# The first branch's half of the output mix in seven block products for eight, with block sums of y made by GpSimd

## The chip, the cores and the metric

The kernel runs on one core of a Trainium2 chip. The metric is the device time of one execution in microseconds (us). A core has five engines that each work through a list of instructions in order and wait for each other by semaphores: TensorE (PE, matrix products; its weight loads are shown as PEld), VectorE (DVE), ScalarE (ACT), GpSimd (POOL) and SyncE (SP, which starts most of the DMA transfers). SBUF is the memory that all of them work on, PSUM the one into which TensorE writes its products.

## The reference

One block of a network on x of 1024 rows by 1024 columns, batch 1. Two attention branches of 512 columns each are projected to 1024 columns, multiplied by gates and added:

```python
h = rms_norm(x, g_pre_mix[l])
proj = h @ w_in[l]
...
gates = jax.nn.sigmoid(proj[..., c1:].astype(jnp.float32)).astype(x.dtype)
gate_sb, gate_diff = jnp.split(gates, N_BRANCHES, axis=-1)
y_sb = stick_breaking_attention(sb_q.reshape(sb_shape), sb_k.reshape(sb_shape), sb_v.reshape(sb_shape))
...
y_diff = (rms_norm(y_diff, w_subln[l]) * (1.0 - lam_init)).reshape(b, s, DIFF_WIDTH)
merged = gate_sb * (y_sb @ w_sb_out[l]) + gate_diff * (y_diff @ w_diff_out[l])
x = x + rms_norm(merged @ w_o[l], g_post_mix[l])
h = rms_norm(x, g_pre_mlp[l])
u = jnp.square(jax.nn.relu(h @ w_up[l]))
x = x + rms_norm(u @ w_down[l], g_post_mlp[l])
```

## The kernel before

**Arithmetic.** All is float32. A product of two float32 matrices is made of three TensorE products of halves: each operand is split into a part `hi`, rounded by ScalarE to the format that TensorE takes (a cast, shown as CAST or COPY), and `lo`, the rest (a subtraction, shown as TENSOR_TENSOR of VectorE); hi·hi, hi·lo and lo·hi are added in PSUM. So every new operand costs one ACT and one DVE instruction before TensorE can use it.

**Stages.** x is normalised and transposed; then come eight attention units, u = 0 to 3 stick-breaking (each two heads) and u = 4 to 7 differential. While a unit's attention runs, a generator (`fill`) hands out other work for TensorE between its blocks: the projections of the next unit and the products of the gates. In the last unit (h = 3, u = 7) this filler is `last_products`: four pairs of gate blocks, each pair as seven block products for eight. A pair needs sums of its weights (`pair_sums`, four GpSimd instructions of 128x512 on the pages `fw`, L593 to L596), their splits (`split_pair`, L603 and L604), and block sums T1 to T4 of the transposed h, which were made in earlier units, stored to DRAM, and are loaded and split here (`split_sum`, L577 and L580). Its products go to the PSUM tiles `g_b`, `g_d`, `g_c` (L547), and VectorE adds them (L631, L641, L645, L649, L653).

In the attention itself, for a block of rows, `z` is the tile of scores (L273, L274); VectorE adds the bias and finds the minimum (`low`, L414), ScalarE takes exponentials, VectorE combines the two maps (`s`, L432), TensorE transposes the result into `tr_df` (L292), ScalarE and VectorE split it into `wth` and `wtl` (L298, L299), and TensorE multiplies by v into `av_d`. At the end of a group of blocks `finish_diff` normalises (`sq`, L387 to L389) and stores y to `y_dram`.

**The mix.** The results y of the units are loaded from `y_dram` as hi and lo. For each of eight blocks b of 128 output columns, `half_mix(b, i, tag)` loads half of the weights (i = 0 for the stick-breaking branch, y 0 to 3; i = 1 for the differential one, y 4 to 7), splits them (`wmix`, L752 and L753), loads the gate, applies its sigmoid (L728), and makes 4 × 3 × 2 = 24 matmuls of 128x512 (L762). 16 halves are 384 matmuls. `merge` multiplies the two by their gates (L773), adds them (L775) and splits the sum for the next stage (L776, L777), the product with w_o (L872).

**The order** on each engine isn't the order of the code: a scheduler that plans with a model of the times sorts the whole program's instructions before it runs. On the chip each engine then keeps to that order. Where a tile goes is set by pools: a tile waits until an older one of its tag and place is done with. The weights of `last_products` and of the mix share the tag `w` with four places, their raw rows the tag `raw` with two.

## Time and profile before

| | |
|---|---|
| three runs | 1453.62, 1453.90 and 1456.99 us, median 1453.9 |
| profiled execution | 1453.24 us, of which the span of the trace is 1451.5 us |
| granted TensorE clock | 0.999 of full speed |
| last attention unit, its second half | 560 to 647 us from the start of the span |
| mix | 647 to 736 us |

A row of the groups on the page reads: line of the kernel, engine, operation, the tile written `<-` the tiles read, shape, count, then busy time, mean length in ns of one, and the engine's idle time just before them with what ended most of it. A row of the timeline has the start in us from the span's start, the length, engine, line, operation, tiles, shape and count, and in brackets the idle time of the engine before it and what released it. A row of the waits has who waited `<-` for what, us in total, number, longest.

### The profile page before, as it was taken

How to read it: one execution, taken by the hardware profiler on the slowest of the kernel's cores; microseconds unless marked ns; L12 is line 12 of the kernel's file. 1: busy time of each engine (PE TensorE's matmuls, PEld its weight loads, DVE VectorE, ACT ScalarE, POOL GpSimd, SP SyncE). 2: the span in 40 equal slices, each digit the busy share in tenths (PEclk: the TensorE clock that was granted, in tenths of full speed). 3: DMA queues.
4: the chain of work that ended last, by engine and by line, in shares of the span. 5: the costliest groups of instructions: out<-in, count | busy, mean ns of one | idle time of the engine just before them, and what ended most of it. 6: DMA issues, size and time to landing. Idle time of an engine off the chain costs nothing. (4 is left out here: it accounts for less than half of the span.)

```text
span 1451.5 us, 19994 instructions
## 1 busy us (share of the span) xinstructions
PE 1425.8 (98%) x7238; PEld 1209.1 (83%) x7238; DVE 1017.3 (70%) x1352; ACT 751.4 (52%) x1325; POOL 388.4 (27%) x377
## 2 busy tenths in 40 slices
PE   7999999999999999999999999999999999999997
PEld 6888998899889888788888878888888888888886
DVE  5477998788657777854755489766664669764783
ACT  6465665666656776444534465444444443534350
POOL 2012322234125002210002334333330357232611
PEclk9999999999999999999999999999999999999999
DMA  5432312222323247475657736544446785678681
GB/s 207 111 94 66 77 48 81 66 73 70 110 94 109 82 153 240 153 277 179 190 167 234 238 129 208 177 159 145 139 159 200 263 276 180 211 236 285 191 288 58
DMA packets 100283, 233.09 MB, mean 161 GB/s; under 512 B 9964, under 2 KB 25560, under 8 KB 100184
## 3 DMA queue, kind: packets, MB, share of 16 engines
q1 hardware_dynamic: 85784, 211.89, 46.2%
q10 hardware_dynamic: 14400, 19.93, 3.8%
q8 instruction: 57, 0.93, 0.3%
q14 instruction: 42, 0.34, 0.1%
HBM read 160.45 MB, written 65.29 MB: 156 GB/s over the span
## 5 line engine op out<-in xcount | busy, mean ns | idle before, releaser
L356 DVE TENSOR_TENSOR_SCAN rest<-rest 128x896 f32<-128x896 f32 (+3 forms) x64 | 88.1, 1385 | 16.4 <-POOL rest L351 15.6
L351 POOL TENSOR_SCALAR_AFFINE_SELECT rest<-rest 128x128 f32<-128x128 f32 x64 | 26.5, 414 | 242.4 <-ACT rest L347 242.4
L762 PE MATMUL mix<-y,wmix 128*128 128x512 f32 x384 | 88.2, 390 | 0.2 <-DMA y<-y_dram 0.2
L762 PEld LDWEIGHTS mix<-y,wmix 128*128 128x128 f32 x384 | 71.9, 188 | 15.4 <-DMA y<-y_dram 0.6
L824 DVE TENSOR_TENSOR lS_lo<-raw_S,lS_hi 128x1024 fp32r<-128x1024 f32 x32 | 53.9, 1683 | 40.1 <-ACT lS_hi L817 40.1
L1170 PE MATMUL dS<-rT_hi,lS_hi 128*128 128x512 f32 x192 | 74.7, 389 | 0.0
L1170 PE MATMUL dS<-rT_lo,lS_hi 128*128 128x512 f32 x192 | 74.7, 389 | 0.0
L1170 PE MATMUL dS<-rT_hi,lS_lo 128*128 128x512 f32 x192 | 74.7, 389 | 0.0
L817 ACT CAST lS_hi<-raw_S 128x1024 fp32r<-128x1024 f32 x32 | 33.6, 1051 | 74.5 <-DMA raw_S<-s_dramS 40.7
L419 ACT ACTIVATE s<-s,low 128x896 f32<-128x896 f32 (+7 forms) x64 | 49.7, 777 | 40.4 <-DVE low L414 40.0
L347 ACT ACTIVATE rest<-z 128x512 f32<-128x512 f32 (+2 forms) x96 | 48.1, 501 | 27.7 <-PE z L274 19.8
L299 DVE TENSOR_TENSOR wtl_sb<-tr_sb,wth_sb 128x512 fp32r<-128x512 f32 (+1 forms) x80 | 48.0, 628 | 8.5 <-ACT wth_sb L298 8.1
L298 ACT CAST wth_sb<-tr_sb 128x512 fp32r<-128x512 f32 (+1 forms) x80 | 41.2, 555 | 24.5 <-PE tr_sb L292 24.1
L351 POOL TENSOR_SCALAR_AFFINE_SELECT beta<-beta 128x128 f32<-128x128 f32 x64 | 52.2, 816 | 2.7 <-ACT beta L348 1.9
L414 DVE CUSTOM_DVE_ANT_0 s<-z,bias 128x512 f32<-128x512 f32 (+3 forms) x64 | 37.3, 586 | 21.1 <-PE z L274 14.9
L207 PE MATMUL acc_gate<-h,hi_gate 128*128 128x512 f32 x128 | 50.6, 396 | 0.0
L208 PE MATMUL acc_gate<-h,lo_gate 128*128 128x512 f32 x128 | 50.5, 394 | 0.0
L206 PE MATMUL acc_gate<-h,hi_gate 128*128 128x512 f32 x128 | 50.4, 394 | 0.0
L994 PE MATMUL c<-hB_lo,wa_hi 128*128 128x512 f32 x128 | 49.9, 390 | 0.0
L994 PE MATMUL c<-hB_hi,wa_hi 128*128 128x512 f32 x128 | 49.9, 390 | 0.0
L1170 PE MATMUL dA<-rB_hi,lA_hi 128*128 128x512 f32 x128 | 49.8, 389 | 0.0
L1170 PE MATMUL dA<-rB_lo,lA_hi 128*128 128x512 f32 x128 | 49.8, 389 | 0.0
(397 smaller groups left out, 4814.1 us busy)
## 6 DMA issues: line engine op xcount, KB each, us to landing
s_dramS<-us SPq DMA_DIRECT2D x64, 256.0 KB, 4.1
raw_S<-s_dramS SPq DMA_DIRECT2D x32, 512.0 KB, 4.1
s_dramA<-u ACTq DMA_DIRECT2D x48, 256.0 KB, 2.3
raw_A<-s_dramA SPq DMA_DIRECT2D x24, 512.0 KB, 4.3
y<-y_dram SPq DMA_DIRECT2D x16, 512.0 KB, 5.2
g<-gate_dram SPq DMA_DIRECT2D x16, 512.0 KB, 4.5
raw_up<-in_w_up_dram SPq DMA_DIRECT2D x16, 512.0 KB, 4.0
up<-in_w_up_dram SPq DMA_DIRECT2D x16, 512.0 KB, 4.0
```

What stands on the lines that cost most here:

```text
L206: nc.tensor.matmul(acc, w_hi[:, ks], b_hi, start=(k == 0), stop=False)
L207: nc.tensor.matmul(acc, w_hi[:, ks], b_lo, start=False, stop=False)
L208: nc.tensor.matmul(acc, w_lo[:, ks], b_hi, start=False, stop=(k == NK - 1))
L299: nc.vector.tensor_tensor(lo[:, :n], tr[:, :n], f32(hi[:, :n]), op=ALU.subtract)
L347: nc.scalar.activation(rest[:, c0:c1], z, AF.Sigmoid, scale=-1.0)
L351: nc.gpsimd.affine_select(tl[:, dg], tl[:, dg], pattern=[[-1, P]], compare_op=ALU.is_gt, fill=fill, base=0, channel_multiplier=1,)
L356: nc.vector.tensor_tensor_scan(back, back, back, 1.0, op0=ALU.mult, op1=ALU.bypass)
L419: e = nc.scalar.activation(s[:, :nk], s[:, :nk], AF.Exp, bias=low, scale=-1.0, accum_out=sums[:, m:m + 1],)
L762: nc.tensor.matmul(accs[c], st, mv[:, cs], start=(first and k == 0), stop=(last and k == 3))
L824: nc.vector.tensor_tensor(lo, raw, f32(hi), op=ALU.subtract)
L994: nc.tensor.matmul(acc, st[:, ks], mv, start=(first and k == 0 and i == 0), stop=(k == 3 and i == 2), skip_group_check=True,)
L1170: nc.tensor.matmul(acc, st[:, e, ts], mv[:, e, :], start=(first and e == 0 and i == 0), stop=(last and e == 1 and i == 2))
```

## The change

Of the first branch's half of the mix, blocks 2 to 7 are made in three pairs, (2, 3), (4, 5) and (6, 7). A pair of blocks is a product of a 2x2 by a 2x2 matrix of blocks (two blocks of output columns, two halves of the 512 inner columns; two halves of the rows), made with seven products of sums in place of eight products. Each of the seven has 2 × 3 = 6 matmuls of 128x512, so a pair has 42 in place of 48. Blocks 0 and 1 and the whole second half stay as they are.

For this, four things are added.

- Each stick-breaking unit also stores its y before the split (`y_raw_dram`, 16 stores of 128 KB).
- `form_y_sums`, called twice in `last_products`, loads these (4 loads of 512 KB), makes four sums each time with GpSimd (8 instructions of 128x512), and stores them to `ty_dram` (8 stores of 256 KB).
- In the mix, `split_ty` loads the sums (8 loads of 256 KB) and splits them; `pair_weights` makes sums of the weights (4 GpSimd instructions of 128x256 a pair) and splits those.
- `pair_products` adds products in PSUM and SBUF with VectorE, and `gated` multiplies by the gates, one product by VectorE and three by GpSimd.

The loads of y 4 to 7, and of all gates but the first two, are put behind the loads of the first pair's weights, and the weights of the first pair and of two second halves are made ahead.

```diff
+            nc.sync.dma_start(out=raw_rows[:, :, j % 2, :], in_=part)
...
+        def form_y_sums(k):
+            if k == 0:
+                page_in["ys"] = pa.tile([P, 4, HALF], F32, tag="v", name="y_sums", bufs=3)
+            ys = page_in["ys"]
+            for j in range(2):
+                nc.sync.dma_start(
+                    out=ys[:, 2 * j:2 * j + 2, :], in_=y_raw_dram[2 * j + k].rearrange("p (c n) -> p c n", c=2)
+                )
+            b11, b12, b21, b22 = (ys[:, i, :] for i in range(4))
+            for name, dst, x0, x1 in (
+                ("T1", b11, b12, b11), ("T3", b12, b22, b12), ("T2", b22, b22, b11), ("T4", b21, b21, b22)
+            ):
+                nc.gpsimd.tensor_tensor(dst, x0, x1, op=ALU.subtract)
+                nc.sync.dma_start(out=ty_dram[name][:, k, :], in_=dst)
...
                 if n < 2:
                     nc.sync.dma_start(out=v, in_=p1_dram[n + 2])
+                    form_y_sums(n)
...
+        def split_ty(name, hi, lo):
+            for k in range(2):
+                nc.sync.dma_start(out=f32(lo[k]), in_=ty_dram[name][:, k, :])
+            for k in range(2):
+                nc.scalar.copy(hi[k], f32(lo[k]))
+                nc.vector.tensor_tensor(lo[k], f32(lo[k]), f32(hi[k]), op=ALU.subtract)
+            ty[name] = hi, lo
...
+        def pair_weights(b):
+            raw = stream.tile([P, 2, HALF], F32, tag="raw", name=f"raw_pair{b}")
+            for e in range(2):
+                last_pair[0] = nc.sync.dma_start(out=raw[:, e, :], in_=w_mix[b + e][:, 0:HALF])
+            wa = wide_tile(f"wa_mix{b}")
+            nc.scalar.copy(wa[:, 0, :], raw[:, 0, :])
+            nc.vector.tensor_tensor(wa[:, 1, :], raw[:, 0, :], f32(wa[:, 0, :]), op=ALU.subtract)
...
+            nc.gpsimd.tensor_tensor(s1, a21, a22, op=ALU.add)
+            nc.gpsimd.tensor_tensor(a21, a11, a21, op=ALU.subtract)
+            nc.gpsimd.tensor_tensor(a11, s1, a11, op=ALU.subtract)
+            nc.gpsimd.tensor_tensor(a12, a12, a11, op=ALU.subtract)
+            hi, lo = (wide_tile(f"w_{n}_mix{b}") for n in ("hi", "lo"))
+            nc.scalar.copy(hi, raw)
+            nc.vector.tensor_tensor(lo, raw, f32(hi), op=ALU.subtract)
+            nc.scalar.copy(w1[:, 0, :], s1)
+            nc.vector.tensor_tensor(w1[:, 1, :], s1, f32(w1[:, 0, :]), op=ALU.subtract)
...
+            product_y(a, first(0), "B11")
+            nc.scalar.copy(v, a)
+            product_y(acc_b, quarter(0, 0), "T2")
+            nc.vector.tensor_tensor(v, acc_b, v, op=ALU.add)
+            product_y(d, quarter(1, 0), "T3")
+            nc.vector.tensor_tensor(q, d, v, op=ALU.add)
+            product_y(a, first(1), "B21", first=False)
+            product_y(c, (w1[:, 0, :], w1[:, 1, :]), "T1")
+            nc.vector.tensor_tensor(q, c, q, op=ALU.add)
+            product_y(d, quarter(1, 1), "T4", first=False)
+            nc.vector.tensor_tensor(r, d, v, op=ALU.add)
+            product_y(c, quarter(0, 1), "B22", first=False)
+            nc.vector.tensor_tensor(v, c, v, op=ALU.add)
+            def gated():
+                g0, g1 = load_gate(b, 0), load_gate(b + 1, 0)
+                left, right = slice(0, HALF), slice(HALF, S)
+                nc.vector.tensor_mul(g0[:, left], a, g0[:, left])
+                nc.gpsimd.tensor_mul(g0[:, right], v, g0[:, right])
+                nc.gpsimd.tensor_mul(g1[:, left], r, g1[:, left])
+                nc.gpsimd.tensor_mul(g1[:, right], q, g1[:, right])
+                return [g0, g1]
...
+        gated = pair_products(2)
         for b in range(NK):
+            if b in (4, 6):
+                gated = pair_products(b)
+            if b > 1 and b % 2 == 0:
+                sbs += gated()
+            df = half_mix(b, 1, ("acc", "sc")[b % 2])
+            merge(b, sbs[b], df)
```

The scheduler sorts the last unit and the mix anew. Three places follow, in the rows of the engines' orders. Lines of the kernel after are 4 higher in this part (L551 for L547).

GpSimd in the last unit, before: the four sums of the second gate pair's weights (`fw1`), then those of the third (`fw2`).

```order
L593 TENSOR_TENSOR page_s1_6563<-fw1_1_6626 128x512
L594 TENSOR_TENSOR fw1_1_6626<-fw1_0_6625,fw1_1_6626 128x512
L595 TENSOR_TENSOR fw1_0_6625<-page_s1_6563,fw1_0_6625 128x512
L596 TENSOR_TENSOR fw1_0_6625<-fw1_0_6625 128x512
L593 TENSOR_TENSOR page_s1_6563<-fw2_1_6716 128x512
```

GpSimd at the same place, after:

```order
L626 TENSOR_TENSOR y_sums_6729<-y_sums_6729 128x512 x3
L597 TENSOR_TENSOR page_s1_6587<-fw1_1_6650 128x512
L626 TENSOR_TENSOR y_sums_6729<-y_sums_6729 128x512
L598 TENSOR_TENSOR fw1_1_6650<-fw1_0_6649,fw1_1_6650 128x512
L599 TENSOR_TENSOR fw1_0_6649<-page_s1_6587,fw1_0_6649 128x512
L600 TENSOR_TENSOR fw1_0_6649<-fw1_0_6649 128x512
L626 TENSOR_TENSOR y_sums_6729<-y_sums_6729 128x512 x4
L597 TENSOR_TENSOR page_s1_6587<-fw2_1_6751 128x512
```

All eight sums of y stand around the second pair's four sums, three ahead of them, one between and four behind.

VectorE in the last unit, before: `page_qu` takes up `g_d` and `g_c` of the first gate pair, `sq` is the normalisation of the unit before, T40 and T41 are the two halves of T4 (their `lo` is made here), and `s_3_0_7` is the last block's map in the last unit.

```order
L387 SCALAR_TENSOR_TENSOR sq_2_0_6418<-ss_2_0_6425,r_2_0_6419 128x512
L580 TENSOR_TENSOR T40_1_6606<-T40_1_6606,T40_0_6605 128x1024
L425 RECIPROCAL sums_3_2_6737<-sums_3_2_6737 128x2
L388 SCALAR_TENSOR_TENSOR sq_2_0_6418<-sq_2_0_6418,r_2_0_6419 128x512
L645 TENSOR_TENSOR page_qu_6564<-g_c0_6661,page_qu_6564 128x512
L580 TENSOR_TENSOR T41_1_6608<-T41_1_6608,T41_0_6607 128x1024
L389 SCALAR_TENSOR_TENSOR sq_2_0_6418<-sq_2_0_6418,r_2_0_6419 128x512
L432 SCALAR_TENSOR_TENSOR s_3_0_7_6375<-s_3_0_7_6375,sums_3_7_6374,s_3_1_7_6387 128x1024
```

VectorE at the same place, after:

```order
L391 SCALAR_TENSOR_TENSOR sq_2_0_6442<-ss_2_0_6449,r_2_0_6443 128x512
L429 RECIPROCAL sums_3_2_6772<-sums_3_2_6772 128x2
L392 SCALAR_TENSOR_TENSOR sq_2_0_6442<-sq_2_0_6442,r_2_0_6443 128x512
L436 SCALAR_TENSOR_TENSOR s_3_0_7_6399<-s_3_0_7_6399,sums_3_7_6398,s_3_1_7_6411 128x1024
L665 TENSOR_TENSOR page_qu_6588<-g_c0_6685,page_qu_6588 128x512
L393 SCALAR_TENSOR_TENSOR sq_2_0_6442<-sq_2_0_6442,r_2_0_6443 128x512
L436 SCALAR_TENSOR_TENSOR s_3_0_2_6773<-s_3_0_2_6773,sums_3_2_6772,s_3_1_2_6780 128x384
L584 TENSOR_TENSOR T40_1_6630<-T40_1_6630,T40_0_6629 128x1024
```

`s_3_0_7` has moved ahead of T40 (and T41, which comes nine rows later still). On TensorE, before, the products with T4 follow those with T1 (T11 is its second half), and the transposes of `s_3_0_7` into `tr_df3_3` come 24 matmuls later:

```order
L547 MATMUL g_c0_6661<-T11_0_6597,page_w1_6565 128x512
L547 MATMUL g_d0_6647<-T40_0_6605,w32_hi0_6617 128x512
L547 MATMUL g_d0_6647<-T40_1_6606,w32_hi0_6617 128x512
L547 MATMUL g_d0_6647<-T40_0_6605,w32_lo0_6618 128x512
L547 MATMUL g_d0_6647<-T40_0_6605,w32_hi0_6617 128x512
```

TensorE at the same place, after:

```order
L551 MATMUL g_c0_6685<-T11_0_6621,page_w1_6589 128x512
L294 MATMUL tr_df3_3_0_6811<-ident_69,s_3_0_7_6399 128x128
L294 MATMUL tr_df3_3_0_6811<-ident_69,s_3_0_6_6370 128x128
L294 MATMUL tr_df3_3_0_6811<-ident_69,s_3_0_7_6399 128x128
L294 MATMUL tr_df3_3_1_6826<-ident_69,s_3_0_7_6399 128x128
L294 MATMUL tr_df3_3_1_6826<-ident_69,s_3_0_6_6370 128x128
L294 MATMUL tr_df3_3_1_6826<-ident_69,s_3_0_7_6399 128x128
L551 MATMUL g_d0_6671<-T40_0_6629,w32_hi0_6641 128x512
L551 MATMUL g_c0_6685<-h110_0_186,w24_hi0_6639 128x512
```

The six transposes have moved to the front; one product with T40 follows, then the twelve with h, and the rest of T4 comes after those.

In the mix, VectorE prepares the second pair's weights (`raw_pair4`, `wa_mix4`, `w1_mix`, `w_lo_mix4`) between gate products (L892, L824) and merges (L908, L910):

```order
L852 TENSOR_TENSOR wa_mix4_7734<-raw_pair4_7731,wa_mix4_7734 128x512
L863 TENSOR_TENSOR w1_mix_7431<-s1_mix4_7737,w1_mix_7431 128x256
L910 TENSOR_TENSOR m_lo0_0_7585<-g_1_0_7400,m_hi0_0_7584 128x512
L892 TENSOR_TENSOR g_2_0_7631<-mixp2_tr0_7501,g_2_0_7631 128x512
L910 TENSOR_TENSOR m_lo1_0_7590<-g_1_0_7400,m_hi1_0_7589 128x512
L794 TENSOR_TENSOR wmix4_1_7811<-raw_mix4_1_7812,wmix4_0_7810 128x512
L861 TENSOR_TENSOR w_lo_mix4_7743<-raw_pair4_7731,w_hi_mix4_7742 128x1024
```

These rows are new; `w_lo_mix4` comes last of the pair's operands, behind a split of other weights (`wmix4`).

More of the change, by code (lines that the diff above doesn't have):

```diff
@@ L141, in hybrid_block_kernel @@
     t_dram = {name: [dram.tile([P, 2, HALF], F32, name=f"{name}_dram{q}") for q in range(2)] for name in ("T1", "T2", "T3", "T4")}
+    y_raw_dram = [dram.tile([P, S], F32, name=f"y_raw_dram{u}") for u in range(N_SB)]
+    ty_dram = {name: dram.tile([P, 2, HALF], F32, name=f"ty_dram{name}") for name in ("T1", "T2", "T3", "T4")}
     p1_dram = dram.tile([4, P, HALF], F32, name="p1_dram")
@@ L726, in load_gate, with load_y @@
             g = pa.tile([P, S], F32, tag="big_s", name=f"g_{b}_{i}", bufs=4)
-            nc.sync.dma_start(out=g, in_=gate_dram[i * NK + b])
+            load = nc.sync.dma_start(out=g, in_=gate_dram[i * NK + b])
+            if i or b > 1:
+                after(load, last_pair[0])
             after(nc.scalar.activation(g, g, AF.Sigmoid), last_exp[0])
             return g
-        y = []
-        for u in range(N_SB + N_DIFF):
+        y7 = pa.tile([P, 2, S], F32R, tag="v", name="y7", bufs=3)
+        y6 = pa.tile([P, 2, S], F32R, tag="v", name="y6", bufs=3)
+        y, ty = [], {}
+        last_pair = [None]
+        def load_y(u):
             if u < 6:
@@ L737, in hybrid_block_kernel @@
             else:
-                both = pa.tile([P, 2, S], F32R, tag="v", name=f"y{u}", bufs=3)
+                both = y6 if u == 6 else y7
                 parts = [both[:, p, :] for p in range(2)]
             for p in range(2):
-                nc.sync.dma_start(out=f32(parts[p]), in_=y_dram[u][:, p, :])
+                load = nc.sync.dma_start(out=f32(parts[p]), in_=y_dram[u][:, p, :])
+                if u > 3:
+                    after(load, last_pair[0])
             y.append(parts)
+        def split_ty(name, hi, lo):
[5 more added lines that the diff above has]
+            ty[name] = hi, lo
@@ L745, in hybrid_block_kernel, with weights_of @@
+        for u in range(4):
+            load_y(u)
+        t2 = pa.tile([P, 2, 2, HALF], F32R, tag="v", name="ty2", bufs=3)
+        split_ty("T2", *([t2[:, p, k, :] for k in range(2)] for p in range(2)))
         m_hi = [[None] * (NK // 2), [None] * (NK // 2)]
         m_lo = [[None] * (NK // 2), [None] * (NK // 2)]
-        def half_mix(b, i, tag):
+        def weights_of(b, i, tiles):
             raw = stream.tile([P, S], F32, tag="raw", name=f"raw_mix{b}_{i}")[:, 0:HALF]
             nc.sync.dma_start(out=raw, in_=w_mix[b][:, i * HALF:(i + 1) * HALF])
-            w = stream.tile([P, 2, HALF], F32R, tag="w", name=f"wmix{b}_{i}", bufs=4)
-            nc.scalar.copy(w[:, 0, :], raw)
-            nc.vector.tensor_tensor(w[:, 1, :], raw, f32(w[:, 0, :]), op=ALU.subtract)
+            hi, lo = tiles
+            nc.scalar.copy(hi, raw)
+            nc.vector.tensor_tensor(lo, raw, f32(hi), op=ALU.subtract)
+            return hi, lo
@@ new lines, in wide_tile, with half_weights, half_mix @@
+        def wide_tile(name, shape=None):
+            return stream.tile(shape or [P, 2, HALF], F32R, tag="w", name=name, bufs=4)
+        ready = {}
+        def half_weights(b, i):
+            if i:
+                tiles = [pa.tile([P, HALF], F32R, tag="small_s", name=f"wmix{b}_{p}", bufs=4) for p in range(2)]
+            else:
+                w = wide_tile(f"wmix{b}")
+                tiles = w[:, 0, :], w[:, 1, :]
+            return weights_of(b, i, tiles)
+        def half_mix(b, i, tag):
+            w_hi, w_lo = ready.pop((b, i), None) or half_weights(b, i)
@@ L758, in half_mix @@
                 y_hi, y_lo = y[4 * i + k]
-                for st, mv, first, last in ((w[:, 0, ks], y_hi, True, False), (w[:, 0, ks], y_lo, False, False), (w[:, 1, ks], y_hi, False, True)):
+                for st, mv, first, last in ((w_hi[:, ks], y_hi, True, False), (w_hi[:, ks], y_lo, False, False), (w_lo[:, ks], y_hi, False, True)):
                     for c in range(2):
@@ new lines, in product_y @@
+        def product_y(acc, w, name, first=True):
+            w_hi, w_lo = w
+            for k in range(2):
+                ks = slice(k * P, (k + 1) * P)
+                b_hi, b_lo = y_block(name, k)
+                for i, (st, mv) in enumerate(((w_hi, b_hi), (w_hi, b_lo), (w_lo, b_hi))):
+                    nc.tensor.matmul(
+                        acc, st[:, ks], mv, start=(first and k == 0 and i == 0), stop=(k == 1 and i == 2),
+                        skip_group_check=True,
+                    )
@@ new lines, in pair_products @@
+        def pair_products(b):
+            wa, hi, lo = ready.pop(b, None) or pair_weights(b)
+            quarter = lambda e, i: (hi[:, e, i * 256:(i + 1) * 256], lo[:, e, i * 256:(i + 1) * 256])
+            first = lambda i: (wa[:, 0, i * 256:(i + 1) * 256], wa[:, 1, i * 256:(i + 1) * 256])
+            a, acc_b, c, d = (
+                ps.tile([P, HALF], F32, tag=tag, name=f"mixp{b}_{tag}{n}", bufs=2) for tag in ("tr", "av") for n in range(2)
+            )
+            v, q = vq[:, 0, :], vq[:, 1, :]
+            product_y(a, first(0), "B11")
[19 more added lines that the diff above has]
+                return [g0, g1]
+            return gated
```

48 lines of the change are left out of this document (31 added, 17 removed).

## Prediction

> **What bounds the kernel now.** I read the page first: busy times, chain, groups.
>
> ```profile
> PE 1425.8 (98%) x7238; PEld 1209.1 (83%) x7238; DVE 1017.3 (70%) x1352; ACT 751.4 (52%) x1325; POOL 388.4 (27%) x377
> PE 40%; DVE 0%; POOL 0%; DVEq 0%; ACT 0%; POOLq 0%; issue 0%; ACTq 0%
> L762 PE MATMUL mix<-y,wmix 128*128 128x512 f32 x384 | 88.2, 390 | 0.2 <-DMA y<-y_dram 0.2
> ```
>
> TensorE (PE) is busy for 98% of the span, and PE is the only engine with a real share of the chain that ended last. The kernel ends when PE has done its matmuls, so two things move the end: matmuls that go, and stretches in which PE waits. The third line is the group the change cuts; PE waits 0.2 us in it.
>
> Next I read PE's waits from 500 to 780 us, which hold the last attention unit (its end) and the mix, and the busy times by stretch. In the second fence the first line names the columns.
>
> ```profile
> PE z L273 <- DVE low L414: 1.0, 1, 1.0
> PE g_b L547 <- DVE page_qu L649: 0.9, 1, 0.9
> PE g_c L547 <- DVE page_qu L645: 0.6, 1, 0.6
> PE g_d L547 <- DVE T L580: 0.3, 1, 0.3
> PE mix L762 <- DMA y<-y_dram: 0.2, 1, 0.2
> ```
>
> ```profile
> core 0: us, PE busy (x) PEld busy (x) DVE busy (x) ACT busy (x) POOL busy (x), PEclk, DMA share, GB/s
> 560.00:600.00 40.00, 37.16 (x177) 30.15 (x177) 37.48 (x63) 30.07 (x51) 8.23 (x4) 1.00 0.55 185
> 646.00:740.00 94.00, 93.84 (x417) 77.47 (x416) 54.95 (x87) 40.45 (x55) 0.00 (x0) 1.00 0.58 187
> ```
>
> From 560 to 600 us PE stands for 40.00 − 37.16 = 2.84 us, VectorE (DVE) is busy for 37.48 of 40, 94%, and all four waits there end on DVE. There PE and DVE share the bound. The mix (646 to 740) is different: PE full, DVE idle for 39 us, GpSimd (POOL) doing nothing. So the change saves matmuls where PE alone decides, and adds GpSimd work where DVE is short.
>
> **The saving.** The program's order of instructions counts 384 matmuls in the mix before and 366 after; all others stay. One stretch of 252 in a row gives the price.
>
> ```profile
> 678.30 57.43 PE L762 MATMUL mix<-y,wmix 128*128 128x512 f32 x252 [0.16 <-DMA y<-y_dram]
> ```
>
> 57.43 / 252 = 0.228 us each; 390 ns in the group is one matmul from start to end, and they overlap. 18 × 0.228 = **4.10 us** gone. The new products have the same tile shape, 128x512, so I take the same price.
>
> **The eight block sums on GpSimd in the last unit.** The order puts them around the four sums of gate weights that the profile shows at 577 us. These and the next pair's first:
>
> ```profile
> 577.01 2.22 POOL L593 TENSOR_TENSOR page_s<-fw 128x512 f32<-128x512 f32 x1 [19.64 <-DVE low L414]
> 579.31 2.16 POOL L594 TENSOR_TENSOR fw<-fw,fw 128x512 f32<-128x512 f32 x1
> 581.55 2.24 POOL L595 TENSOR_TENSOR fw<-page_s,fw 128x512 f32<-128x512 f32 x1
> 583.87 1.60 POOL L596 TENSOR_TENSOR fw<-fw 128x512 f32<-128x512 f32 x1
> 601.70 1.29 POOL L593 TENSOR_TENSOR page_s<-fw 128x512 f32<-128x512 f32 x1 [16.23 <-DMA fw<-in_w_in_dram]
> ```
>
> And DVE in the same time:
>
> ```profile
> 576.85 1.22 DVE L580 TENSOR_TENSOR T<-T,T 128x1024 fp32r<-128x1024 f32 x1
> 578.54 1.77 DVE L580 TENSOR_TENSOR T<-T,T 128x1024 fp32r<-128x1024 f32 x1
> 580.24 0.68 DVE L641 TENSOR_TENSOR page_qu<-g_d,page_v 128x512 f32<-128x512 f32 x1
> 581.43 1.21 DVE L580 TENSOR_TENSOR T<-T,T 128x1024 fp32r<-128x1024 f32 x1
> 582.64 1.70 DVE L388 SCALAR_TENSOR_TENSOR sq<-sq,r 128x512 f32<-128x512 f32 x1
> 584.27 0.68 DVE L645 TENSOR_TENSOR page_qu<-g_c,page_qu 128x512 f32<-128x512 f32 x1
> 584.87 1.69 DVE L580 TENSOR_TENSOR T<-T,T 128x1024 fp32r<-128x1024 f32 x1
> 586.48 0.68 DVE L389 SCALAR_TENSOR_TENSOR sq<-sq,r 128x512 f32<-128x512 f32 x1
> 587.08 1.27 DVE L432 SCALAR_TENSOR_TENSOR s<-s,sums,s 128x1024 f32<-128x1024 f32 x1
> ```
>
> A sum takes 1.29 us alone and up to 2.24 here, and DVE pays too: 1.77 and 1.69 where 1.22 is usual, and 1.70 in L388 where the like L389 takes 0.68. That is 0.55 + 0.47 + 1.02 = 2.04 us for four sums, 0.51 each. The operations at 580.24 and 584.27, which read one operand from PSUM, are not lengthened.
>
> Eight more sums at 0.51 take 4.1 us of DVE in a stretch where DVE has 2.5 us to spare and PE already waits for it. Bounds: 0, if the sums fall into DVE's gaps or beside its PSUM operations; 8 × 1.29 = 10.3, if each stands in DVE's way for its whole length. I take **4.1 us**, as the nearest rows measure just this pairing, and let PE pay it all, since what DVE is late with is what PE waits for.
>
> The Trainium skill, "SBUF — State Buffer", section "Who interferes with whom", has a rule against this change: VectorE and GpSimd share a port pair, and a VectorE operation with two SBUF inputs and a GpSimd operation that reads SBUF exclude each other, the second waiting until the first has ended. By the rule alone the term would lie at its upper bound, 10.3 us. The trace agrees on who collides (one PSUM operand, no lengthening), but shows 0.51 a sum on the average, as some sums wait for DVE and others find it at a free operation.
>
> What is queued behind: the order moves `s_0_7` (L432 above) ahead of both halves of T4, and PE's six transposes of it ahead of T4's products. PE reaches that place here:
>
> ```profile
> 582.01 0.39 PE L547 MATMUL g_d<-T,w_hi 128*128 128x512 f32 x1
> 582.70 0.50 PE L547 MATMUL g_d<-T,w_hi 128*128 128x512 f32 x1 [0.29 <-DVE T L580]
> 585.00 0.73 PE L547 MATMUL g_c<-h,w_hi 128*128 128x512 f32 x2 [0.64 <-DVE page_qu L645]
> 580.79 1.04 ACT L577 CAST T<-T 128x1024 fp32r<-128x1024 f32 x1
> 581.72 1.15 ACT L431 ACTIVATE s<-s,sums 128x1024 f32<-128x1024 f32 x1
> ```
>
> Put at 581.43, where T now stands, L388 takes 0.68 or 1.70, then `s_0_7` 1.27 or, blocked once, 1.27 + 1.02 = 2.29: it ends between 583.4 and 585.4, and its input from ScalarE is there by 582.9. So the transposes wait for 1.4 to 3.4 us in one go, where T4 waited for 0.29 and g_c for 0.64. Behind them T4's halves, the attention's second parts and the next scores wait for DVE in their turn. This is where the 4.1 us should show; it is not added to them.
>
> **The mix.** Added on GpSimd are 12 sums of 128x256, at half of 1.29 some 0.65 us each (an estimate), and 9 gate products of 128x512: 12 × 0.65 + 9 × 1.29 = 19.4 us. At 0.51 each these 21 take at most 10.7 us of DVE, and DVE's 17 more operations (0.68 to 1.27) some 14 (17 × 0.8, an estimate): 25 us in the 39 it has idle, so they hide. What may not hide is the second pair's weights. Its half pages share four buffers with the pair before it, and DVE's order has the wide subtraction (`w_lo_mix`) late, behind gate products and merges.
>
> ```profile
> raw_mix<-in_w_mix_dram SPq DMA_DIRECT2D x14, 256.0 KB, 4.0
> ```
>
> The chain is load 4.0, three of the four sums 2.0, cast 1.04 as in the row of 580.79, subtraction 1.22: 8.2 us. Between the first pair's last product and the second's first stand 72 matmuls, 16.4 us. That covers the chain, but not certainly the queues in front of it. Bounds 0 and 8.2; nearest is a wait of about one DVE operation, **1.0 us**. The third pair has 33 and 9 more matmuls ahead, and I give it nothing.
>
> **Transfers.**
>
> ```profile
> DMA packets 100283, 233.09 MB, mean 161 GB/s; under 512 B 9964, under 2 KB 25560, under 8 KB 100184
> ```
>
> 36 more (16 stores of y's raw rows, 4 loads and 8 stores for the sums, 8 loads of the sums), 8 MB beside 233. The DMA engines are busy for 0.55 and 0.58 in the two stretches; the sums are stored near 590 us, the mix begins at 647. Nothing, unless a load of a sum stands ahead of something urgent on SP; bounds 0 and 4.0, one such load.
>
> **Sum**, against the profiled execution (1453.24 us, span 1451.5): 1453.24 − 4.10 + 4.1 + 1.0 = **1454.2 us**. That execution lies 0.7 below the median of the three runs, 1453.9; I leave this in the scatter.
>
> **Rivals.**
>
> *The sums are hidden.* GpSimd stands idle for 19.64 us ahead of 577.01; if the sums run early, or DVE's gaps take them, DVE loses nothing and PE gains its 18 matmuls: 1453.24 − 4.10 = 1449.1. For it speaks that the order has three sums ahead of L593; against it that DVE is 94% busy in the stretch and that the other five stand behind. Chance 0.18.
>
> *Each sum blocks DVE as L388 was blocked.* That is 1.02 us apiece, 8.2 in all: 1453.24 − 4.10 + 8.2 + 1.0 = 1458.3, slower, and up to 1460.4 at 1.29 apiece. The place is the last unit from 565 to 600; it decides from 1.02 a sum, twice what the four cost. For it: L388's row, and DVE operations with two SBUF inputs follow each other there. Against: two of three lengthened rows lost only half. The rule of the Trainium skill above is this case. Chance 0.16.
>
> *The mix turns into the wait.* If the weights of the second and third pair come late by half their chain, 4.1 us twice, PE waits 8.2 instead of 1.0: 1461.4. Against it: 16.4 us of matmuls ahead. Chance 0.08.
>
> That the change does not do what it says is excluded for the count (366 in the order).
>
> **How the numbers follow.** The forecast has 0.58, with 1451.5 to 1457.5 of its own (last unit 1.4 to 7.4). The range reaches to the first rival's time, 1449.1, and to the top of the second, 1460.4; outside are a part of the first and the third. Against 1453.9, 0.3% (4.4 us, about what a measurement of this kernel can tell from no change) means below 1449.5 or above 1458.3. Faster: two thirds of the first rival, 0.12. Slower: the third, three quarters of the second, and a tail of 0.04 of the forecast, 0.24. Within: 0.64.
>
> **What would show it.** The 366 matmuls at 0.228 us; PE's waits from 560 to 600 grown from 2.84 to about 7 us, the longest a wait of the transposes for `s_0_7`; DVE rows of 1.7 us where 0.68 or 1.22 is usual, eight sums with lengths between 1.29 and 2.24; in the mix one wait of about 1 us ahead of a product with the second pair's `w_lo_mix`. Waits in 560 to 600 unchanged at 3 us would say that the sums are hidden; mix waits above 3 us, or any for a load of y's sums, would make the prediction wrong in a place that I count as covered.

## The result, and the profile after

| | before | after |
|---|---|---|
| median, range | 1454.22 us (1453.62 to 1457.45, 5 runs) | 1464.91 us (1464.04 to 1466.19, 5 runs) |
| ratio of the times, 95% interval | | 1.0065 [1.005, 1.0079] |
| profiled execution, its span | 1453.24, 1451.5 us | 1466.19, 1464.5 us |

The kernel became slower by 0.65%, and 1464.9 lies above the range (1449.1 to 1460.4). The profiled execution is the slowest of the five, with a granted clock of 0.995; the quickest, 1464.04 us, had 0.998, so the clock's part below is likely at its largest there. The matmuls are gone as counted. On the page after, the lines of busy time and of the mix's ordinary products (240 of them; 126 are in the pairs, 366 together):

```profile
PE 1430.1 (98%) x7220; PEld 1208.7 (83%) x7220; DVE 1047.0 (71%) x1369; ACT 760.7 (52%) x1339; POOL 427.5 (29%) x406
L821 PE MATMUL mix<-y,wmix 128*128 128x512 f32 x240 | 58.0, 395 | 1.1 <-ACT wmix L793 1.1
```

TensorE has 18 matmuls fewer and is "busy" for 4.3 us longer: the same matmuls take longer somewhere. One place stands in the second row: an ordinary product of the mix has a mean length of 395 ns, where it had 390. PE's waits from 500 to 800 us, after (who waited, for what, us in total, number, longest):

```profile
PE tr_df L294 <- DVE s L436: 3.7, 1, 3.7
PE trh L1039 <- ACT ht L1045: 2.1, 2, 1.4
PE mix L821 <- ACT wmix L793: 1.1, 1, 1.1
...
PE mixp_tr L840 <- ACT w_hi_mix L860: 0.3, 1, 0.3
...
```

And the stretches of the last unit, the mix and the w_o product (columns as in the prediction; the number behind POOL's is the granted clock), first before, then after:

```profile
560.00:646.00 86.00, 83.17 (x417) 69.25 (x417) 68.92 (x123) 51.01 (x93) 18.86 (x12) 1.00 0.61 205
735.57:851.91 116.34, 116.22 (x545) 96.65 (x544) 66.05 (x72) 53.06 (x103) 26.13 (x40) 1.00 0.67 217
```

```profile
560.00:646.00 86.00, 79.82 (x384) 65.86 (x384) 72.83 (x120) 51.37 (x94) 31.60 (x20) 0.96 0.66 216
646.00:740.00 94.00, 92.51 (x406) 74.70 (x405) 67.29 (x98) 46.32 (x66) 24.21 (x20) 1.00 0.70 241
742.53:864.67 122.14, 117.81 (x545) 95.92 (x544) 69.27 (x74) 53.08 (x103) 25.60 (x40) 1.00 0.63 207
```

Three things stand in them. In the last unit PE is idle for 86.00 − 79.82 = 6.18 us, where it was 2.83. In the same 86 us the mean clock is 0.96, where it was 1.00; 4% of 86 is some 3.4 us, a loss that looks like busy time. And in the w_o stage, which the prediction does not speak of, PE is idle for 122.14 − 117.81 = 4.33 us against 0.12.

Where each stage begins on TensorE, from the timeline, gives the balance. The last unit and the mix are taken together, as the first products of the mix stand among the unit's last ones and their number there differs.

| us | before | after | difference |
|---|---|---|---|
| start of span to first `g_b` of the last unit | 571.7 | 572.3 | +0.6 |
| to the first `o` (w_o): last unit and mix | 163.9 | 170.2 | +6.3 |
| to the first `p_sc` (w_up) behind it: w_o | 116.3 | 122.1 | +5.8 |
| to the end | 599.6 | 599.8 | +0.2 |

If the second row holds the forecast saving of 4.1 us, 10.4 us were lost in it: 3.35 of waits and 3.4 of clock in the last unit, 1.33 of waits in the mix (94.00 − 92.51 = 1.49 against 0.16), and 1.7 because the saving is smaller, as the next rows show; some 0.6 us stay unassigned. The third row is the second large loss.

**The price of a matmul.** Two runs of the mix's ordinary products in PE's timeline after, both at a granted clock of 1.00 and with no wait inside:

```profile
661.76 6.51 PE L821 MATMUL mix<-y,wmix 128*128 128x512 f32 x28
678.70 16.96 PE L821 MATMUL mix<-y,wmix 128*128 128x512 f32 x72
```

The next matmuls start at 668.11 and 695.49. So a product of the first branch's half (the first row) takes 6.35 / 28 = 0.227 us, as in the run of 252 before (57.27 / 252 from start to start), and one of the second branch's half takes 16.79 / 72 = 0.233. The 366 products together take 85.1 us from start to start without idle time, the 384 before 87.5: 2.4 us are saved in place of 4.1. Why is open. The weights of the second half lie in tiles of another tag after the change (`small_s` for `w`), and no run changed that back.

**The wait of 3.7 us.** GpSimd after, a group of sums in each row:

```profile
577.83 3.53 POOL L626 TENSOR_TENSOR y_sums<-y_sums 128x512 f32<-128x512 f32 x2 [2.74 <-DMA y_sums<-y_raw_dram]
581.32 2.27 POOL L597 TENSOR_TENSOR page_s<-fw 128x512 f32<-128x512 f32 x1
583.55 1.27 POOL L626 TENSOR_TENSOR y_sums<-y_sums 128x512 f32<-128x512 f32 x1
...
586.57 2.15 POOL L599 TENSOR_TENSOR fw<-page_s,fw 128x512 f32<-128x512 f32 x1
```

DVE beside it:

```profile
578.30 1.91 DVE L584 TENSOR_TENSOR T<-T,T 128x1024 fp32r<-128x1024 f32 x1
580.68 1.76 DVE L584 TENSOR_TENSOR T<-T,T 128x1024 fp32r<-128x1024 f32 x1
582.36 0.68 DVE L661 TENSOR_TENSOR page_qu<-g_d,page_v 128x512 f32<-128x512 f32 x1
583.67 1.70 DVE L392 SCALAR_TENSOR_TENSOR sq<-sq,r 128x512 f32<-128x512 f32 x1
585.29 2.28 DVE L436 SCALAR_TENSOR_TENSOR s<-s,sums,s 128x1024 f32<-128x1024 f32 x1
```

These four DVE rows with two operands in SBUF lost 0.69, 0.54, 1.02 and 1.01 us against 1.22, 1.22, 0.68 and 1.27; `page_qu` with one operand in PSUM lost nothing. `s_0_7` ends at 587.57, not at 583.4 to 585.4 as forecast: it begins later, and both it and L392 ahead of it met a sum.

**The slow clock.** PE behind that wait:

```profile
587.63 1.54 PE L294 MATMUL tr_df<-ident,s 128*128 128x128 f32 x6 [3.71 <-DVE s L436]
589.39 1.05 PE L551 MATMUL g_c<-h,w_hi 128*128 128x512 f32 x2
592.26 0.62 PE L551 MATMUL g_c<-h,w_hi 128*128 128x512 f32 x2
```

Two products take 1.05 us at 589 and 0.62 at 592. The granted clock in the trace is either 1.00 or 0.50, and the slow stretches inside the kernel last 3.41 us, or twice that. The two of the last unit stand here, each with the 3.41 us ahead of it (columns as above):

```profile
584.26:587.67 3.41, 0.04 (x1) 0.04 (x1) 3.41 (x3) 1.88 (x3) 3.33 (x3) 1.00 0.81 271
587.67:591.08 3.41, 3.41 (x11) 2.95 (x12) 3.41 (x4) 2.12 (x3) 3.33 (x3) 0.50 0.47 124
597.92:601.33 3.41, 1.65 (x7) 0.88 (x6) 3.41 (x6) 1.51 (x4) 0.00 (x0) 1.00 0.25 66
601.33:604.74 3.41, 3.39 (x14) 3.20 (x14) 3.41 (x8) 1.30 (x3) 0.00 (x0) 0.50 0.86 281
```

Half the clock for 3.41 us is worth up to 1.7 us of work, so the two make up the 3.4. PE was idle for 3.37 us of the 3.41 ahead of the first, and for 1.76, in two waits of about 0.9, ahead of the second. Before had no wait over some 1.0 us from 500 to 800 and no slow stretch there. The Trainium skill, "TensorE: Matmul & The Clock Gate", section "Why this matters for your kernels", says it as a rule: no idle gaps of TensorE over some 3 us between bursts, or the clock falls to half; the section "What's actually happening" calls the window in which activity is counted free-running. The trace agrees with the rule at 588 us: 3.7 us of idling, then 0.50. At 601 us it differs: no single wait of 3 us was needed.

### The profile page after: what moved, and what is told of

It reads as the page before. It is cut to its first block, busy times and chain, and to the rows that moved or that the text cites. A ratio compares the mean times of both kernels' runs of the same rounds, so it can differ in the third digit from the quotient of the medians.

```text
span 1464.5 us, 20152 instructions
## 1 busy us (share of the span) xinstructions
PE 1430.1 (98%) x7220; PEld 1208.7 (83%) x7220; DVE 1047.0 (71%) x1369; ACT 760.7 (52%) x1339; POOL 427.5 (29%) x406
## 4 chain that ended last, share of the span: by engine, by line
PE 82%; DVE 6%; DMA 4%; issue 3%; ACT 2%; POOL 1%; SPq 0%; DVEq 0%; POOLq 0%; ACTq 0%
PE dS L1311 12%; PE dA L1311 9%; PE p_tr L1135 5%; PE p_av L1135 5%; PE c L1135 4%; PE o L1013 3%; PE p_sc L1135 3%; PE mix L821 2%; PE acc_gate L209 2%; PE acc_gate L208 2%; PE acc_gate L210 2%; PE z L276 2%; PE z L275 2%; PE tr_sb L294 2%; PE c L551 2%
## 5 line engine op out<-in xcount | busy, mean ns | idle before, releaser
L821 PE MATMUL mix<-y,wmix 128*128 128x512 f32 x240 | 58.0, 395 | 1.1 <-ACT wmix L793 1.1
L821 PEld LDWEIGHTS mix<-y,wmix 128*128 128x128 f32 x240 | 45.0, 188 | 12.1 <-ACT wmix L793 1.5
L965 DVE TENSOR_TENSOR lA_lo<-raw_A,lA_hi 128x1024 fp32r<-128x1024 f32 x24 | 37.1, 1545 | 21.2 <-ACT lA_hi L958 19.7
```

What stands on the lines that cost most here:

```text
L821: nc.tensor.matmul(accs[c], st, mv[:, cs], start=(first and k == 0), stop=(last and k == 3))
L965: nc.vector.tensor_tensor(lo, raw, f32(hi), op=ALU.subtract)
```

## The experiments

The theory at the start: the eight sums in the last unit cost the waits there and, by them, the clock; what the w_o stage loses comes from the pairs in the mix. Rivals: the unit's loss comes from the new order (transposes first), or the w_o loss from the sums too. Each ratio is to the kernel before, timed on the same chip. "Unit + mix" and "w_o" are the stretches of the table above (163.9 and 116.3 before). "PE idle" is for 560 to 646 and for 646 to 740 us, from the busy times (2.83 and 0.16 before). The last three columns are of one execution each, the profiled one, the median is of all.

| run | median us | ratio [95%] | unit + mix | w_o | PE idle |
|---|---|---|---|---|---|
| after | 1464.91 | 1.0065 [1.005, 1.0079] | 170.2 | 122.1 | 6.18, 1.49 |
| no_sums | 1461.34 | 1.0039 [1.0027, 1.0051] | 165.8 | 123.0 | 3.70, 3.01 |
| sums_alone | 1463.3 | 1.0059 [1.0047, 1.0071] | 170.8 | 116.8 | 7.67, 1.14 |
| sums_early | 1467.48 | 1.008 [1.0066, 1.0095] | 169.9 | 122.4 | 5.70, 2.70 |
| sums_late | 1463.93 | 1.0055 [1.0043, 1.0068] | 171.9 | 123.5 | 4.37, 5.32 |
| small_store | 1461.1 | 1.0039 [1.0025, 1.0053] | 170.2 | 120.2 | 6.41, 1.30 |
| small_store_before | 1453.88 | 0.9991 [0.9982, 1.0] | 164.2 | 116.0 | 2.86, 0.42 |
| two_pairs | 1456.26 | 1.0004 [0.9994, 1.0015] | 163.9 | 119.3 | 3.69, 0.75 |
| five_rows | 1458.8 | 1.0022 [1.001, 1.0034] | 166.7 | 118.8 | 5.50, 0.00 |
| five_rows_before | 1454.74 | 0.9991 [0.9981, 1.0] | 164.3 | 117.5 | 2.81, 0.63 |
| sums_dve_rows | 1460.42 | 1.0033 [1.0024, 1.0042] | 168.3 | 117.7 | 4.42, 3.74 |
| five_rows_no_sums | 1458.58 | 1.0017 [1.0006, 1.0028] | 166.1 | 117.7 | 3.67, 3.39 |
| two_pairs_rows | 1457.14 | 1.0003 [0.9992, 1.0014] | 166.3 | 118.3 | 3.67, 2.51 |

### The sums: without them, alone, earlier, later

**no_sums**, the changed kernel:

```diff
-                nc.gpsimd.tensor_tensor(dst, x0, x1, op=ALU.subtract)
```

> The changed kernel without the eight GpSimd sums in the last unit: the rows of y are loaded and stored in place of the sums, so the pairs of the mix work on blocks that aren't sums. All transfers, the order of the transposes ahead of T4's products and the whole mix stay. In the profile of the changed kernel the last unit lost about 7 us against before (3.3 more of waits, 3.4 by a granted clock of 0.96 from 560 to 646 us), the mix waited for about 2.5 us, and the stage of w_o lost 5.7. Theory (GpSimd against VectorE, and then a slow clock behind the long wait): the wait of the transposes falls from 3.7 to about 1.4 us, the clock stays at 1.00, the last unit loses at most 1 us against before; mix and w_o as they were: about 1458. Rival (the new order of the last unit is what costs): the last unit still loses 5 us or more, about 1464. Rival (w_o's loss is a consequence of the last unit's): it goes too, about 1452.

**sums_alone**, the kernel before with the stores of y, `form_y_sums` and its two calls, their results unused:

```diff
+            nc.sync.dma_start(out=raw_rows[:, :, j % 2, :], in_=part)
...
+                    form_y_sums(n)
```

> The kernel before with the stores of y's rows and the eight GpSimd sums in the last unit added, and nothing that uses them: the mix has its 384 matmuls and its old form. Theory: the last unit loses 7 us as in the changed kernel, the mix and w_o nothing: about 1461. Rival (w_o's loss follows the last unit's): w_o loses some 6 us more, about 1467. Rival (the last unit's loss is due to something that the mix starts early, its loads of y and of the sums): the last unit loses less than 3 us, below 1457.

Without the sums the last unit idles for 3.70 us, 0.87 more than before, at a clock of 1.00; with them alone it idles for 7.67, and its waits are the ones of after. So the theory holds for the unit. Both times are above what was expected: no_sums because the mix idles longer (3.01 us), sums_alone (1463.3 for 1461) for a reason that its profile, of its quickest execution (1460.89 us), does not show. PE's waits, no_sums, then sums_alone:

```profile
PE trh L1038 <- ACT ht L1044: 3.0, 1, 3.0
PE g_d L551 <- DVE T L584: 1.9, 2, 1.1
PE tr_df L294 <- DVE s L436: 1.8, 1, 1.8
PE mixp_av L839 <- DVE vq_mix L879: 1.5, 1, 1.5
PE mixp_tr L839 <- DVE w_lo_mix L860: 1.1, 1, 1.1
```

```profile
PE tr_df L294 <- DVE s L436: 3.4, 1, 3.4
PE g_d L551 <- DVE T L584: 2.4, 2, 1.5
```

The transposes come first in no_sums too and wait for 1.8 us there, so the new order accounts for that part and the sums beside DVE for the rest of the 3.7. `trh` waits for `ht` in no_sums and not in sums_alone (w_o 123.0 against 116.8), so the w_o loss belongs to the mix in pairs; of no_sums' 6.7 us some 1.7 are a stretch of 3.41 us at half the clock behind that wait (at 785 us). In sums_alone the wait of 3.4 us was not followed by a slow clock:

```profile
585.46 0.87 PE L294 MATMUL tr_df<-ident,s 128*128 128x128 f32 x6 [3.44 <-DVE s L436]
```

Six transposes took 0.87 us here and 1.54 in after. The reason stands in the trace. The slow stretches of an execution lie on a grid of 3.41 us; sums_alone has one later, from 863.67 us, and counted back from it in steps of 3.4133 us the wait falls into two stretches, about half into each:

```profile
580.37:583.78 3.41, 1.64 (x8) 1.02 (x6) 3.41 (x5) 2.79 (x5) 3.41 (x3) 1.00 0.58 163
583.78:587.20 3.42, 1.74 (x11) 1.58 (x12) 3.42 (x4) 1.33 (x4) 3.34 (x3) 1.00 0.94 343
```

PE was idle for 1.77 us of the first and 1.67 of the second, and no slow stretch followed; in after the wait covered one stretch whole. The traces of the other runs agree, from 500 to 1000 us: ahead of every drop the 3.41 us had at least 1.66 us of idling (one 1.40), and none without a drop had more than 1.84. So the border is near half a stretch, and where the grid lies in an execution decides about a wait of this length.

**sums_early** calls `form_y_sums` from the filler of the unit before; **sums_late** puts the sums behind the last gate pair's weight sums:

```diff
+                if u == N_SB + 2 and cost in (0, 15):
+                    form_y_sums(cost // 15)
```

> The changed kernel with the eight GpSimd sums a unit earlier, in the third differential unit, where VectorE is busy for about 65%. Theory: that unit has room, so the sums cost nothing there; the last unit is near the time of before, mix and w_o as in the changed kernel: about 1458. Splits of the sums that now can be made in the last unit may cost it 1 to 2 us on VectorE. Rival (sums on GpSimd cost PE 7 us wherever they stand): about 1464.

```diff
-                nc.gpsimd.tensor_tensor(dst, x0, x1, op=ALU.subtract)
+                after(nc.gpsimd.tensor_tensor(dst, x0, x1, op=ALU.subtract), last_sum[0])
```

> The changed kernel with the eight GpSimd sums behind the last of the gate weights' sums, in the last 25 us of the last unit, where VectorE was busy for 68% and PE waited for nothing before. The transposes stay ahead of T4's products. Theory: the first pairs of the last unit are as in the run without sums, so the transposes wait for about 2 us and the clock stays at 1.00; the last unit loses 2 us at most instead of 8; the mix may wait some 3 us more for the sums, that come late; w_o keeps its loss: about 1460. Rival (GpSimd sums in the last unit cost it 5 us wherever they stand): about 1464.

Neither helps. In sums_early the unit before loses what it did not lose (a wait of 1.8 us for `wtl_df` at 520 us; PE idles for 1.87 us from 500 to 560, where before does not at all), two splits of the sums move into the tight stretch of the last unit (VectorE at 583.0 and 586.9 us, in after at 611.4 and 612.6), and that unit keeps idling for 5.70 us. The time, 1467.5, is above the theory's 1458 and the rival's 1464; four stretches of 3.41 us at half the clock, from 521 to 869 us, are in it. In sums_late the last unit is nearly back (4.37 us, transposes 2.4), and the mix pays: 5.32 us of idling, at a mean clock of 0.96. The median is the 1464 of the rival, but not for its reason, as the last unit idles for 1.5 us more than before and not for 5; the profiled execution took 1468.49 us, 4.6 more than the median. PE's waits, sums_late:

```profile
PE mixp_tr L842 <- ACT vq_mix L878: 2.4, 2, 1.4
PE tr_df L294 <- DVE s L436: 2.4, 1, 2.4
```

### The w_o stage: what the write of a row waits for

ScalarE copies the product `o` into a row `or`, VectorE and ScalarE make h of it, TensorE transposes h (`trh`), ScalarE copies that out (`ht`). ACT before, then ACT and PE after, at the third row block (timeline):

```profile
776.44 0.60 ACT L109 ACTIVATE or<-o 128x512 f32<-128x512 f32 x1 [2.70 <-DMA x_dram<-xr]
```

```profile
786.75 0.60 ACT L109 ACTIVATE or<-o 128x512 f32<-128x512 f32 x1 [4.47 <-DMA x_dram<-xr]
787.90 1.07 ACT L1045 COPY ht<-trh 128x512 f32<-128x512 f32 x2
788.54 1.14 PE L1039 MATMUL trh<-ident,or 128*128 128x128 f32 x8 [1.45 <-ACT ht L1045]
```

The write waits until the second store of x has left its place among the `row` tiles, `ht` stands behind the write in ACT's order, and PE waits for `ht`. From the store's issue (772.60 before, 781.13 after) to the write it is 3.8 us before and 5.6 after. The theory then: the store lands late because loads of `xr` (512 KB each) now go out beside it; before, one is issued 1.2 us ahead of it and one 1.7 us behind, after, 1.2 us ahead and 0.3 behind.

**small_store** stores 64 of the 1024 columns, and the last stage reads x in place of that store's result:

```diff
-        nc.scalar.dma_start(out=x2_dram[t * P:(t + 1) * P, :], in_=xt)
+        nc.scalar.dma_start(out=x2_dram[t * P:(t + 1) * P, 0:DH], in_=xt[:, 0:DH])
```

> The changed kernel with one transfer of the w_o stage cut: of each tile of 128 rows of x behind the first half, only 64 of 1024 columns are stored, and the last stage reads x in its place. In the changed kernel w_o lost 5.7 us: there the second of these stores and a load of x start 0.3 us apart (1.7 before), the store lands after 5.5 us (3.7 before), ScalarE waits for the page that it frees, and PE for ScalarE's copy of the transposes. Theory: with a small store the page is free early, the wait of the transposes for ht goes and w_o gets back 4 us or more: about 1460. Rival (the preparation of w_o, its loads and splits, is late by itself): w_o keeps a loss of 3 us or more, about 1464.

Its control, on the kernel before:

> The same cut in the kernel before, the control: its store of 3.7 us was on time, so both theories expect w_o within 1 us of before, about 1454. If it gains 3 us or more, the gain of the other run is not evidence for the collision.

The stage loses 3.9 us in place of 5.8 (120.2 against 116.3). It gets 1.9 us back where the theory said 4 or more, and what it still loses is within the rival's bound of 3 or more. The write still started only 5.5 us behind the store's issue, as ACT's row shows, with a load issued 0.1 us ahead of the store:

```profile
788.91 0.60 ACT L109 ACTIVATE or<-o 128x512 f32<-128x512 f32 x1 [4.40 <-DMA x_dram<-xr]
```

So the size of the store was the wrong thing to change. **five_rows** takes the wait itself away, by a fifth place for the rows:

```diff
-        return pb.tile(shape or [P, S], dt, tag="page", name=name, bufs=24)
+        return pb.tile(shape or [P, S], dt, tag="page", name=name, bufs=23)
...
-        return pb.tile(shape or [P, S], F32, tag="row", name=name, bufs=4)
+        return pb.tile(shape or [P, S], F32, tag="row", name=name, bufs=5)
```

> The changed kernel with one more place for the rows of the w_o stage (five in place of four) and one page less, so that ScalarE's write of row block 2 no longer waits until the second store of x has left its page. If the store that lands late is what the w_o stage loses, the write starts some 3 us earlier, ht of row block 1 with it, and the stage takes at most 2 us more than before the change in place of 6: about 1460 against 1465. If the preparation in front of that stage is late in itself (the rival), the stage still loses 4 us or more and the time stays at 1463 to 1466.

> The same edit on the kernel before, the control: the row's wait costs it little, since the store lands in 3.7 us there; 1453 to 1455 by either theory. A gain here would say that the edit helps whatever the change did.

The write starts at once, and PE's next `trh` waits for less:

```profile
778.13 0.59 ACT L109 ACTIVATE or<-o 128x512 f32<-128x512 f32 x1
783.24 1.06 PE L1039 MATMUL trh<-ident,or 128*128 128x128 f32 x8 [0.68 <-DVE or L1031]
```

The time falls to 1458.8 us, ratio 1.0022 against 1.0065 without the edit; the control gains nothing that can be measured (0.9991, its interval ends at 1.0). The write is 38.7 us behind the stage's start, in after 44.2. The stage takes 118.8 us, 3.3 less; 2.5 more than before, of which the control shows 1.2 as well. The edit also lets the scheduler move `trh` on TensorE, here four products forward, in the control likewise, so the wait is not all that it changes. Unit and mix fell too, by 3.5 us, though TensorE's order is the same there in both kernels; 2.2 us of it are idling (5.50 and 0.00 against 6.18 and 1.49). Why is open: it may be how the two profiled executions differ. So of the 6 us between the two medians only the stage's 3.3 are put down to the wait.

### The mix: fewer pairs, and both causes out

**two_pairs** has no sums and makes blocks 6 and 7 as before (372 matmuls, 2.74 us saved at the forecast's price):

```diff
-            if b in (4, 6):
+            if b == 4:
...
+            if b > 5:
+                sbs.append(half_mix(b, 0, ("tr", "av")[b % 2]))
```

> The changed kernel without the GpSimd sums (y's rows are stored in their place, so the pairs work on blocks that aren't sums), and with the third pair of blocks (6, 7) made by ordinary half products: 12 matmuls fewer than before instead of 18, and the tail of the mix as before. In the run without sums the mix lost 5.2 us of waits and w_o 6.6. Theory (the third pair's sums, gates and merges at the mix's end push the preparation of w_o behind PE): w_o within 2 us of before, the mix loses its wait of 1.3 us for the third pair's weights; the time is 1454 + 0.6 + 4 + 2 - 2.7, about 1458, and 4 us better than the run without sums. Rival (any of the pairs' work brings w_o out of step): w_o still loses 5 us or more, about 1463.

It takes 1456.26 us, less than either expectation. The w_o stage loses 2.9 us, more than the 2 of the theory and less than the 5 of the rival. So the third pair accounts for a part of that stage's loss, and the time is that of the kernel before.

**five_rows_no_sums** joins the edits of no_sums and five_rows, **two_pairs_rows** those of two_pairs and five_rows:

> Both causes out at once: no sums of y in the last unit (the first two raw rows of y stand in for them in the stores, so the output is not the reference's) and five rows in the w_o stage. If the two causes are separate and together the whole loss, what is left is near the time before, 1454 to 1457 (ratio 0.999 to 1.001): the saving of 4.1 us is eaten by waits in the mix for the pairs' weights. If something else is lost as well (the rival), the time stays at 1459 or more.

> The same with two pairs in place of three (blocks 6 and 7 ordinary, 372 matmuls in the mix, 2.74 us saved). It shows the most that the pairs can bring when the sums cost nothing: by the theory 1452 to 1455 (ratio 0.997 to 0.9995), a little under the kernel before; if the waits of the mix belong to the first pairs already (the rival), the same as or above the kernel before.

Both missed their expectation; two_pairs_rows, with 1.0003, came out as its rival said, the same as the kernel before. With both causes out of three pairs 1458.58 us are left, a ratio of 1.0017, where 0.9972 would be the forecast saving alone. The mix has taken over. PE's waits in five_rows_no_sums:

```profile
PE mixp_av L839 <- DVE vq_mix L879: 1.8, 1, 1.8
PE mixp_tr L839 <- DVE w_lo_mix L860: 1.3, 1, 1.3
```

In this kernel PE idles for 3.39 us from 646 to 740, in five_rows, the same kernel with the sums, for 0.00. With the sums the last unit ends later, and the first pair's adds and the second pair's weights are ready when PE comes; without them PE comes earlier and waits for these. What was won in the last unit (5.50 − 3.67 = 1.8 us of idling, and the clock) went back in the mix. With two pairs the same add is waited for (0.75 us of idling in two_pairs, 2.51 in two_pairs_rows); the time is that of the kernel before, 1.0004 and 1.0003, with the fifth row or without.

Its rows show why the add is late. The product to be copied ended at 661 us; ScalarE's copy of it comes at 663.86, behind two sigmoids of the gates, and VectorE's adds behind more (timeline, rows of ACT, DVE and PE):

```profile
661.95 2.01 ACT L750 ACTIVATE g<-g 128x1024 f32<-128x1024 f32 x2
663.86 0.57 ACT L875 COPY vq_mix<-mixp_tr 128x512 f32<-128x512 f32 x1
664.85 1.28 DVE L823 TENSOR_TENSOR g<-mix,g 128x512 f32<-128x512 f32 x2
...
666.64 0.75 DVE L394 SCALAR_TENSOR_TENSOR y<-y,subln,sq 128x512 f32<-128x512 f32 x1
667.31 0.69 DVE L877 TENSOR_TENSOR vq_mix<-mixp_tr,vq_mix 128x512 f32<-128x512 f32 x1
668.10 0.69 DVE L879 TENSOR_TENSOR vq_mix<-mixp_av,vq_mix 128x512 f32<-128x512 f32 x1
668.84 0.73 PE L839 MATMUL mixp_av<-tyT,w_hi_mix 128*128 128x512 f32 x2 [1.80 <-DVE vq_mix L879]
```

Gate products, a weight split and the normalisation of the last unit's y come first, and PE may add T4's product to that PSUM tile only when the add has read it.

### The sums on VectorE

**sums_dve_rows** is complete: five rows, and the sums on VectorE behind the last gate pair's weight splits.

```diff
-                nc.gpsimd.tensor_tensor(dst, x0, x1, op=ALU.subtract)
+                after(nc.vector.tensor_tensor(dst, x0, x1, op=ALU.subtract), last_sum[0])
```

> The changed kernel complete, with the eight sums of y made by VectorE behind the last gate pair's weight splits (600 to 625 us), where GpSimd has no sums of its own to collide with, and five rows in the w_o stage. If the loss of the last unit came from GpSimd's sums beside VectorE's tight stretch, the unit takes at most 2 us more than before, the transposes' wait falls below 2 us, and the time is 1455 to 1459. If eight sums cost 5 us wherever they stand at this end of the unit (the rival), about 1460 to 1464.

The last unit's part came out: it idles for 1.6 us more than before, where 2 at most was expected. The transposes' wait, 2.2 us, missed its bound of 2 narrowly, and the time lies in the rival's range. One of VectorE's sums in the timeline, then the longest waits of PE:

```profile
607.88 0.69 DVE L626 TENSOR_TENSOR y_sums<-y_sums 128x512 f32<-128x512 f32 x1
```

```profile
PE tr_df L294 <- DVE s L436: 2.2, 1, 2.2
PE mixp_tr L842 <- ACT w_hi_mix L862: 1.4, 1, 1.4
```

A sum costs 0.69 us of VectorE where GpSimd takes 1.27 and disturbs others, the last unit idles for 4.42 us in place of 6.18, the clock stays at 1.00. Again the mix takes it back, with 3.74 us. The ratio, 1.0033, is not better than that of five_rows (1.0022); the intervals overlap. No version beat the kernel before.

## Why the prediction was wrong

- **The saving, −4.10 us**: right in count (366), wrong in price. "The same tile shape, 128x512, so I take the same price" does not hold: the second half's ordinary products take 0.233 us each in place of 0.227, and 2.4 us are saved in place of 4.1. No variant with three pairs has unit and mix below 165.8 us, where 163.9 − 4.1 = 159.8 would be the forecast saving alone.
- **The eight sums, +4.1 us**: the mechanism was right, and the place: DVE operations with two SBUF operands lengthened, others not, the transposes of `s_0_7` the longest wait. The size of the waits was near: 3.35 us more in after, 4.84 more in sums_alone. From 560 to 600 us PE idled for 5.26 us, where about 7 was forecast. The transposes' own wait, 1.4 to 3.4 us forecast, was 3.71. What the term left out is that idling has a price of its own: two stretches at half the clock, 3.4 us in the profiled execution. The forecast put the wait at up to 3.4 us and asked nothing about the clock, though it had the granted clock in every row.
- **The mix, +1.0 us, with the third pair at nothing**: too small, and argued from the wrong thing. The forecast compared the second pair's chain of 8.2 us with 16.4 us of matmuls, and VectorE's 25 us with 39 idle ones. It left out that a pair's own adds stand between its products (`vq_mix`) in an in-order queue. Where PE comes in time it idles for 3.0 to 3.7 us in the mix (no_sums, five_rows_no_sums, sums_dve_rows). In after itself only 1.49, as the late last unit hides it; that this lies near the forecast is luck, for the one wait of 1.1 us there was for ordinary weights (`wmix`), and the second pair's cost 0.3. The rival "the mix turns into the wait" is this case at a smaller size.
- **Everything else, nothing**: the step that failed most. The stage behind the mix lost 5.8 us. The forecast looked at transfers in the last unit and in the mix and named no term for w_o, whose chain (write of a row, store, `ht`, `trh`) had no slack: PE waited for 0.12 us there, and ACT already stood for 2.70 us for a store. 3.3 us of the 5.8 are shown to be that wait (five_rows). Why the stage's preparation runs 1 to 2 us later against PE than before, so that the store meets a load, was read off the traces and not tried; the other 2.5 us stay open.
- **The terms were added as if they were separate.** They are not: the sums cost 0.0026 of the time between after and no_sums, 0.0059 alone, and 0.0005 between five_rows and five_rows_no_sums (this last is within the intervals). What one stage gives back the next takes, as its operands are no earlier.

No rival was right. The third, 1461.4, comes nearest in time, but by luck: it has 8.2 us of waits in the mix, where after had 1.5. The second (1458.3 to 1460.4) has the loss in the right unit, about as large as the waits and the clock there together, but by 1.02 us a sum and not by the clock. None had a term for w_o.

## What to carry to other kernels

Fewer matmuls are worth their time only if every stage behind them has its operands earlier too; ask of each following stage what its first wait would be if TensorE came 4 us sooner, or the preparation 2 us later, and read the idle time of the other engines' in-order queues for it (ACT's 2.70 us for a store was the warning). Idling has a price beyond itself, and short waits close together pay it too: behind 3.41 us of which PE was idle for about half or more, in one wait or in two of 0.9 us, the clock was halved for the next 3.41 us. Read the price of a matmul again in the profile after; the same shape took 0.227 and 0.233 us in one kernel. Where a small elementwise operation must be added beside a busy VectorE, compare it on VectorE itself (0.69 us) with GpSimd (1.27 us, and up to 1.02 us for whoever it meets); here the last unit gained by it, and the whole kernel did not.
